# Three feed-forward stages whose down projections take seven half-block products instead of eight

## The chip, the cores and the metric

One core of a Trainium2 chip runs the whole program. The metric is the device time of one execution in microseconds, the median of three runs. A profile of one more execution shows when each engine was busy: PE (TensorE's matmuls), PEld (its weight loads), DVE (VectorE), ACT (ScalarE), POOL (GpSimd) and the DMA queues, of which SP issues most.

## The reference

Two transformer-like blocks on 512 tokens of width 1024, all in float32: first a block with convolution, stick-breaking and cross attention and a feed-forward part, then an attention layer, a convolutional feed-forward layer, a state-space layer and a second convolutional feed-forward layer. The change touches the second matrix of the three feed-forward parts:

```python
# first block: D_FF = 4096
x = x + jnp.square(jax.nn.relu(h2 @ w_up[l])) @ w_down[l]
# each convolutional feed-forward layer: D_FF_2 = 2816
gate, up = jnp.split(h @ w_in, [D_FF_2], axis=-1)
gate = causal_dwconv(gate, conv_w, conv_b)
return (jax.nn.silu(gate) * up) @ w_out
```

## The kernel before

**Matmuls in three parts.** A float32 product is made of three matmuls on rounded halves: each operand is split into a high part (a cast on ScalarE: `act.copy`) and a low part (a subtraction on VectorE: `dve.tensor_sub`), and high*high, high*low and low*high are summed in PSUM. Weights are split on the fly: a load of 1 MB lands in one of two `raw` buffers, and chunks of 128x512 become pairs `whi`, `wlo` in rings of nine (`WB = 9`). So each weight chunk costs one ScalarE and one VectorE instruction of 128x512, beside its matmuls.

**Jobs.** The program is a list of jobs, each a stretch of matmuls. `jobA` makes 256 features for all 512 tokens (48 matmuls), `projB` makes 512 output columns for all tokens out of jobs of four weight chunks (`jobB`: for each tile of 128 tokens, for each k, three matmuls). `run_jobs` goes through the jobs; at each `yield` of a job it emits the low halves that are due (`split_lo`), perhaps the next chunk's high half (`more`, at a rate that `speed` sets, while fewer than nine chunks are in use) and the tasks that are due by a clock of planned times (`pump`). The order in each engine's queue is the order of emission. Tasks are spawned with planned delays and planned engine costs.

**The feed-forward stages.** The first block has four groups of 8 feature tiles (128 features each), each convolutional layer groups of 8, 8 and 6. A group's features come from `jobA`s: in the first block 4 per group, in a convolutional layer 4 (or 3) pairs, one job for the gate and one for the other factor. Each feature tile is 128x512 (features by tokens); `Feat.put` splits it into high and low. The down projection of group g is placed after the first `jobA` (the first pair) of group g+1; the last group's stands at the stage's end, where the normalisation of the next stage hangs on it (`x_done`: sums of squares on ScalarE, transposes on PE, copies on VectorE and ScalarE). It is eight half-block products in effect: 2 column halves, 4 token tiles, 8 (or 6) feature tiles, three matmuls each; each of the two halves ends with four adds of a PSUM bank into the residual `x`.

GpSimd does one product by a 128x512 row per gate tile (`fy<-fy,R`), and little else in these stages.

Of the kernel before, what the change touches and what calls it, by code (L numbers as in the profile page):

```python
# [10 lines left out]
F32R = mybir.dt.float32r  # L11
# [45 lines left out]
class Job:  # L57
    def __init__(self, pieces, nk, nc, run, pre=None):
        self.pieces = pieces
        self.nk = nk  # L60
        self.nc = nc
        self.run = run
        self.pre = pre
        self.speed = 0.6


@with_exitstack
def kernel(ctx: ExitStack, tc: tile.TileContext, ins: dict, out: bass.AP, parts=(1, 2, 3, 4, 5)):
# [107 lines left out]
    def rel(tag):  # L176
        freed[tag].append(max(done[0], now[0]))

    def hand_over():

        live["g"] -= 1
        live["t"] += 1

    def u8(nm, dt=F32):
        return up.tile([128, 2048], dt, tag="u8", name=nm)

    def t2(nm, dt=F32, n=512):
        return tp.tile([128, n], dt, tag="t2", name=nm)
# [49 lines left out]
    def drain():  # L238
        while tasks:
            step()  # L240

    def until(ready):

        limit = now[0] + 500.0
        while not ready():
            if tasks:
                step()
            else:
                now[0] += 0.1
            assert now[0] < limit  # L250
# [39 lines left out]
    WB = 9  # L290

    def load(i):
        if i >= len(jobs) or i in raws:
# [9 lines left out]
    def split_hi(i, c):  # L303

        j = jobs[i]
        if c == 0:
            load(i)
            load(i + 1)
        r = raws[i].rearrange("p k c -> p (k c)")
# [3 lines left out]
        s = r[:, c * w:(c + 1) * w]  # L313
        act.copy(h, s)
        late.append(lambda: dve.tensor_sub(l, s, f(h)))
        split.setdefault(i, []).append((h, l))
        if (c + 1) * w >= j.nk * j.nc:
            raws.pop(i)

    def split_lo():  # L320
        while late:
# [2 lines left out]
    class W:  # L324
# [3 lines left out]
        def get(self, k, c0, c1):  # L328
# [3 lines left out]
            o = (k % kq) * j.nc  # L332
            return h[:, o + c0:o + c1], l[:, o + c0:o + c1]

    def run_jobs():
        chunks = [(i, c) for i, j in enumerate(jobs) for c in range(max(1, j.nk * j.nc // 512))]
        st = {"n": 0, "used": 0}

        def more(limit, upto=None):
            while limit > 0 and st["n"] < len(chunks):  # L340
                i, c = chunks[st["n"]]
                if upto is not None and i > upto:
                    return
                if upto is None and st["used"] >= WB:
                    return
                split_lo()
                split_hi(i, c)
                st["n"] += 1
                st["used"] += 1
                limit -= 1  # L350

        for i, j in enumerate(jobs):
            if j.pre is not None:
                j.pre()
            more(99, i)
            if late and chunks[st["n"] - 1][0] == i:
# [9 lines left out]
            st["used"] -= len(split.pop(i))  # L366
        drain()

    def mm3(ps, sh, sl, mh, ml, first, last):
# [4 lines left out]
    class Feat:  # L374
# [136 lines left out]
    def projB(wap, r0, nk, c0, X, evac, ntt=NT, pre=None, k0=0, cut=None, mid=None):  # L511
        state = {}
        n = 0
        for m in cut or [4] * (nk // 4):
            jobB(wap, r0 + n * 128, m, c0, X, k0 + n, state, n == 0, n + m == nk, evac, ntt, 512,
                 pre if n == 0 else mid)
            n += m


    def rstd_of(ms, n, nm):  # L520
# [40 lines left out]
    def x_half(tt, h):  # L561
        return x_ap(tt)[:, h * 512:(h + 1) * 512]
# [51 lines left out]
    def between(holder):  # L614
        return lambda: holder["row"]()
# [18 lines left out]
    def first_block():  # L634
# [422 lines left out]
        def up_evac(g, k0):  # L1057
            def evac(ft, ps):
                if k0 + ft == 0:
                    F[g] = Feat("ff", KD)  # L1060
                r = t2("r")
                dve.scalar_tensor_tensor(out=r, in0=ps, scalar=0.0, in1=G["R"], op0=ALU.max, op1=ALU.mult)

                def rest():
                    act.activation(out=r, in_=r, func=AF.Square)
                    yield from F[g].put(k0 + ft, r)

                spawn(rest(), 0.8)
            return evac

        def down(g, last):
            for half in range(2):
                projB(ins["w_down"], g * 1024, KD, half * 512, lambda: F[g], residual(half, last),
                      pre=(lambda: hooks.update(x=hooks["next1"])) if last and half == 0 else None)

        for g in range(4):
            for i in range(4):
                jobA(ins["w_up"], g * 1024 + i * 256, lambda: G["h"], up_evac(g, 2 * i),
                     between=between(G) if g == 0 and i == 0 else None)
                if i == 0 and g > 0:  # L1080
                    down(g - 1, False)
        down(3, True)
# [212 lines left out]
    def conv_ffn(layer, G, nxt):  # L1295
        w = ins["ffn_w_in_2"][layer]
        wo = ins["ffn_w_out_2"][layer]
        F = {}
        gt = {}

        def gate_evac(k0):
            def evac(ft, ps):
                k = k0 + ft

                def done(y):
                    pool.tensor_tensor(out=y, in0=y, in1=G["R"], op=ALU.mult)
                    gt[k] = y

                spawn(conv_silu(ps, G["R"], [col(f"fcw{layer}", 3 * k + i) for i in range(3)],
                                col(f"fcb{layer}", k), None, done))  # L1310
                pump()
            return evac

        def up_evac(k0, g, base):
            def evac(ft, ps):
                k = k0 + ft
                if k == base:
                    F[g] = Feat("fs", 8)
                until(lambda: k in gt)
                y = gt.pop(k)  # L1320
                dve.tensor_mul(y, ps, y)
                spawn(F[g].put(k - base, y), 0.9)
            return evac

        def down(g, base, nk, last):
            for half in range(2):
                projB(wo, base * 128, nk, half * 512, lambda: F[g], residual(half, last),
                      cut=[nk - 4, 4],
                      pre=(lambda: hooks.update(x=hooks[nxt])) if last and half == 0 else None)

        groups = ((0, 8), (8, 8), (16, 6))
        X = lambda: G["h"]
        for g, (base, n) in enumerate(groups):
            for i in range(n // 2):
                k0 = base + 2 * i
                jobA(w, k0 * 128, X, gate_evac(k0), between=between(G) if k0 == 0 else None)
# [425 lines left out]
```

## Time and profile before

| | |
|---|---|
| Median of three runs | 2547.79 us (2546.73 to 2548.28) |
| Profiled execution, its own time | 2546.88 us |
| Its span, first to last instruction | 2544.8 us |
| Mean granted TensorE clock | 0.995 |
| PE busy | 98% of the span, 11732 matmuls |
| DVE, ACT, POOL busy | 59%, 41%, 10% |

Busy times of an engine are unions of its instructions. A chain of waits is followed back from the last instruction. An engine that is off the chain may still decide when others can start.

### The profile page before, as it was taken

What the parts mean: (1) busy time and instruction counts of PE and PEld (TensorE: products, weight loads), DVE (VectorE), ACT (ScalarE), POOL (GpSimd) and SP (SyncE); (2) the same over time, 40 slices, a digit from 0 to 9 for tenths busy, and PEclk for the clock granted to TensorE, in tenths of its full rate; (3) what the DMA queues carried; (4) which work ended last, traced back from release to release, by engine and by line L of the source; (5) the groups of instructions that cost most, each with busy time, mean ns of one, the idle gap of its engine ahead of it and who ended that gap; (6) DMA issues with size and microseconds to landing.
All of it is one profiled execution on the core that took longest, in us unless ns stands there. A gap on an engine that the chain in (4) does not pass through costs nothing.

```text
span 2544.8 us, 30656 instructions
## 1 busy us (share of the span) xinstructions
PE 2494.2 (98%) x11732; PEld 2015.6 (79%) x11732; DVE 1509.6 (59%) x2752; ACT 1054.7 (41%) x2242; POOL 253.0 (10%) x292
## 2 busy tenths in 40 slices
PE   8999999999999999999898999999999998999999
PEld 6777777788888888888676888888778886888887
DVE  6435679953445443346867654646688687764644
ACT  6444565632224332234555332223565544432321
POOL 1000111201110000002210110100011011110100
PEclk9999999999999999999999999999999998999999
DMA  5212222233232332332121232322332431322232
GB/s 203 100 66 87 96 67 67 67 124 102 90 134 94 103 99 83 99 100 75 44 100 34 96 103 83 116 75 93 114 96 83 124 108 58 100 95 90 98 100 83
DMA packets 197394, 238.54 MB, mean 94 GB/s; under 512 B 5856, under 2 KB 148576, under 8 KB 197248
## 3 DMA queue, kind: packets, MB, share of 16 engines
q1 hardware_dynamic: 194224, 230.17, 27.7%
q10 hardware_dynamic: 3024, 6.42, 0.7%
q8 instruction: 92, 1.51, 0.2%
q14 instruction: 54, 0.44, 0.1%
HBM read 232.31 MB, written 4.26 MB: 93 GB/s over the span
## 4 chain that ended last, share of the span: by engine, by line
PE 91%; DVE 6%; ACT 1%; issue 1%; DMA 1%; POOL 1%; SPq 0%; ACTq 0%; DVEq 0%; POOLq 0%
PE ga L83 48%; PE gb L83 33%; PE y L83 1%; PE z L83 1%; PE as L83 1%; PE tr L88 1%; PE o L83 1%; DVE wlo L116 1%; PE aT L88 1%; DVE ae L116 1%; DVE sm L116 1%; DVE fy L116 1%; PE xs L83 1%; PE xo L83 1%; PE ao L83 0%
## 5 line engine op out<-in xcount | busy, mean ns | idle before, releaser
L116 DVE TENSOR_TENSOR wlo<-raw,whi 128x512 fp32r<-128x512 f32 (+1 forms) x813 | 578.7, 735 | 220.5 <-ACT whi L116 219.8
L83 PE MATMUL ga<-hh,whi 128*128 128x512 f32 x1672 | 668.0, 400 | 0.0
L83 PE MATMUL ga<-hh,wlo 128*128 128x512 f32 x1672 | 652.9, 390 | 2.1 <-DVE wlo L116 2.1
L83 PE MATMUL ga<-hl,whi 128*128 128x512 f32 x1672 | 652.1, 390 | 0.0
L116 ACT CAST whi<-raw 128x512 fp32r<-128x512 f32 (+1 forms) x813 | 479.1, 616 | 317.1 <-PE gb L83 212.2
L83 PEld LDWEIGHTS ga<-hh,wlo 128*128 128x128 f32 x1672 | 313.6, 188 | 70.4 <-DVE wlo L116 2.9
L83 PEld LDWEIGHTS ga<-hh,whi 128*128 128x128 f32 x1672 | 313.9, 188 | 68.9 <-issue 4.4
L83 PEld LDWEIGHTS ga<-hl,whi 128*128 128x128 f32 x1672 | 313.9, 188 | 66.3 <-issue 2.2
L116 DVE TENSOR_TENSOR x<-gb,x 128x512 f32<-128x512 f32 x136 | 93.9, 690 | 274.4 <-PE gb L83 273.1
L83 PE MATMUL gb<-whi,hh 128*128 128x512 f32 (+1 forms) x416 | 169.5, 408 | 0.0
L83 PE MATMUL gb<-whi,hl 128*128 128x512 f32 (+1 forms) x416 | 159.4, 383 | 0.0
L83 PE MATMUL gb<-wlo,hh 128*128 128x512 f32 (+1 forms) x416 | 159.1, 382 | 0.3 <-DVE wlo L116 0.3
L83 PE MATMUL gb<-whi,fsh 128*128 128x512 f32 x352 | 137.7, 391 | 0.0
L83 PE MATMUL gb<-whi,fsl 128*128 128x512 f32 x352 | 137.0, 389 | 0.0
L83 PE MATMUL gb<-wlo,fsh 128*128 128x512 f32 x352 | 137.0, 389 | 0.0
L116 ACT ACTIVATE fy<-fy,cols 128x512 f32<-128x512 f32 x60 | 43.5, 725 | 183.6 <-DVE fy L116 183.6
L116 POOL TENSOR_TENSOR fy<-fy,R 128x512 f32<-128x512 f32 x44 | 62.1, 1411 | 575.6 <-ACT fy L116 570.0
L116 DVE SCALAR_TENSOR_TENSOR fy<-fg,cols,fy 128x510 f32<-128x510 f32 (+1 forms) x136 | 104.6, 769 | 4.8
L83 PE MATMUL gb<-whi,ffh 128*128 128x512 f32 x256 | 100.4, 392 | 0.0
L83 PE MATMUL gb<-whi,ffl 128*128 128x512 f32 x256 | 99.7, 389 | 0.0
L83 PE MATMUL gb<-wlo,ffh 128*128 128x512 f32 x256 | 99.7, 389 | 0.0
L116 DVE TENSOR_TENSOR fg<-ga,R 128x512 f32<-128x512 f32 x68 | 46.6, 685 | 84.4 <-PE ga L83 73.5
(271 smaller groups left out, 3703.3 us busy)
## 6 DMA issues: line engine op xcount, KB each, us to landing
raw<-in_ffn_w_in_dram SPq DMA_DIRECT2D x44, 1024.0 KB, 4.9
raw<-in_w_in_dram SPq DMA_DIRECT2D x40, 1024.0 KB, 4.9
raw<-in_ffn_w_out_dram SPq DMA_DIRECT2D x20, 1024.0 KB, 4.9
raw<-in_w_up_dram SPq DMA_DIRECT2D x16, 1024.0 KB, 5.3
raw<-in_w_down_dram SPq DMA_DIRECT2D x16, 1024.0 KB, 4.9
raw<-in_ssm_w_in_dram SPq DMA_DIRECT2D x16, 1024.0 KB, 5.0
raw<-in_attn_w_in_dram SPq DMA_DIRECT2D x9, 1024.0 KB, 5.0
raw<-in_w_mem_kv_dram SPq DMA_DIRECT2D x8, 1024.0 KB, 5.1
```

Source lines behind the costliest of these rows:

```text
L83: nc.tensor.matmul(o, lhsT=lhsT, rhs=rhs, **kw)
L88: nc.tensor.transpose(o, i, idn)
L116: return fn(*args, **kw)
```

## The change

Each group's down projection is written as a product of 2x2 blocks: tokens in halves of 256 (two tiles), features in halves of nk/2 tiles, columns in halves of 512. Seven products of half blocks give the four output blocks, with sums and differences of blocks as operands. Each product is 4 (or 3) feature tiles by 2 token tiles by three matmuls.

- `seven` replaces the two `projB` of a group by seven jobs. The four quarter blocks of the weight are loaded once, two into `raw`, two into buffers of the `u8` pool (`big`). After a chunk of product 0, 1, 2 or 3 is split, a sum of 128x512 of two quarter blocks is made in place (`j.after = mix(...)`), so that a later product finds its operand there. All 7x4 (7x3) chunks are split into high and low.
- `Hidden` replaces `Feat` for the features: they are kept unsplit, and `operands` makes each product's left operand in two tasks, one per pair of feature tiles: for four of the seven a sum of 128x512, for all seven a cast on ScalarE and a subtraction on VectorE of 128x512. At most three operands stand at a time (`NOP`). `work()` spawns them at the start of the `jobA` (the pair) that precedes the down projection.
- Sums go through `add_on`, which takes GpSimd unless, by planned times, VectorE would be free more than 1 us earlier (`lighter(pool, dve, 1.0)`).
- After each product two PSUM banks (256 tokens by 512 columns) are added into `x`: seven times two adds per group, where there were eight. Banks are kept over several products.

```diff
+def lighter(a, b, more):
+    return b if max(b.free, now[0]) + more < a.free else a
...
         act.copy(h, s)
         late.append(lambda: dve.tensor_sub(l, s, f(h)))
+        if j.after is not None:
+            late.append(lambda: j.after(c))
...
+    SEVEN = (("11", "e"), ("s1", "c"), ("s2", "e"), ("s4", "c"), ("s3", "e"), ("12", "f"), ("22", "e"))
+    NOP = 3
+    def add_on(out, a, b, op):
+        lighter(pool, dve, 1.0).tensor_tensor(out=out, in0=a, in1=b, op=op)
...
+        def operands(self, a, b):
...
+                while self.done < i - (NOP - 1) or not all(
+                        ("r", k + j * self.hk) in self.got for j in need for k in range(a, b)):
+                    yield 0.3
...
+                if name == "s1":
+                    add_on(t, A(2, 1), A(2, 2), ALU.add)
+                elif name == "s2":
+                    add_on(t, t, A(1, 1), ALU.subtract)
+                elif name == "s4":
+                    add_on(t, A(1, 2), t, ALU.subtract)
+                elif name == "s3":
+                    add_on(A(2, 1), A(1, 1), A(2, 1), ALU.subtract)
...
+                act.copy(h, src)
+                yield 0.2
+                dve.tensor_sub(r3(o[:, 1024 + a * 256:1024 + b * 256], b - a), src, f(h))
...
+    def seven(wap, r0, nk, H, last, pre=None):
...
+        def first(i):
+            load(i)
+            R["0"] = flat(raws.pop(i))
+            load(i + 1)
+            R["1"] = flat(raws.pop(i + 1))
+            big("2", 2, 2)
+        def mix(out, a, b):
+            return lambda c: add_on(*[R[x][:, c * 512:(c + 1) * 512] for x in (out, a, b)], ALU.subtract)
...
+                for n, (k, t) in enumerate(order):
+                    wh, wl = wt.get(k, 0, 512)
+                    h, l = H().at(name, k)
+                    h, l = (x[:, t * 128:(t + 1) * 128] for x in (h, l))
+                    ps = banks[bk, t]
+                    s, e = new and k == 0, k == hk - 1
+                    pe.matmul(ps, lhsT=h, rhs=wh, start=s, stop=False, skip_group_check=True)
+                    pe.matmul(ps, lhsT=h, rhs=wl, start=False, stop=False, skip_group_check=True)
+                    pe.matmul(ps, lhsT=l, rhs=wh, start=False, stop=e, skip_group_check=True)
...
+                for t in range(2):
+                    tt = 2 * (row - 1) + t
+                    xa = x_half(tt, half)
...
+                    dve.tensor_add(xa, banks[bk, t], xa)
...
+                    if fin and last:
+                        x_done(tt, half)
+                yield
...
+        srcs = ("0", "0", "0", "2", "1", "3", "0")
+        sums = (("0", "1", "0"), ("0", "2", "0"), ("1", "2", "1"), ("0", "3", "0"), None, None, None)
...
+            j.speed = 1.2
...
-                    yield from F[g].put(k0 + ft, r)
+                    act.activation(out=F[g].slot(k0 + ft), in_=r, func=AF.Square)
...
         def down(g, last):
-            for half in range(2):
-                projB(ins["w_down"], g * 1024, KD, half * 512, lambda: F[g], residual(half, last), ...
+            seven(ins["w_down"], g * 1024, KD, lambda: F[g], last, ...
...
-                dve.tensor_mul(y, ps, y)
-                spawn(F[g].put(k - base, y), 0.9)
+                dve.tensor_mul(F[g].slot(k - base), ps, y)
+                F[g].got.add(("r", k - base))
```

## Rows read from the trace of the kernel before

**Rows 1.** The page's first part: busy us, share of the span, instructions.
```profile
PE 2494.2 (98%) x11732; PEld 2015.6 (79%) x11732; DVE 1509.6 (59%) x2752; ACT 1054.7 (41%) x2242; POOL 253.0 (10%) x292
```
**Rows 2.** The chain of waits in order of time: start us, us, what.
```profile
859.00 43.52 PE gb L83 x192
902.52 43.52 PE ga L83 x192
...
2464.38 43.52 PE ga L83 x192
2507.90 32.65 PE gb L83 x144
2540.58 0.69 DVE x L116
```
**Rows 3.** Busy us by stretch (x instructions), then PEclk, DMA share, GB/s.
```profile
core 0: us, PE busy (x) PEld busy (x) DVE busy (x) ACT busy (x) POOL busy (x), PEclk, DMA share, GB/s
859.00:902.50 43.50, 43.50 (x193) 36.02 (x193) 15.93 (x25) 12.17 (x20) 0.00 (x0) 1.00 0.25 82
902.50:946.00 43.50, 43.50 (x194) 36.02 (x193) 20.00 (x31) 16.07 (x28) 0.00 (x0) 1.00 0.35 111
1109.00:1158.00 49.00, 49.00 (x239) 40.78 (x238) 25.20 (x42) 18.53 (x40) 1.36 (x3) 1.00 0.27 90
1559.00:1646.00 87.00, 87.00 (x386) 72.03 (x385) 54.61 (x79) 25.79 (x45) 11.22 (x8) 1.00 0.32 105
```
**Rows 4.** Timeline of DVE around a gate job and its partner: start us, us.
```profile
1556.17 0.69 DVE L116 TENSOR_TENSOR x<-gb,x 128x512 f32<-128x512 f32 x1 [1.43 <-PE gb L83]
1556.78 1.29 DVE L116 TENSOR_TENSOR wlo<-raw,whi 128x512 fp32r<-128x512 f32 x2
...
1564.33 0.69 DVE L116 TENSOR_TENSOR fg<-ga,R 128x512 f32<-128x512 f32 x1 [4.15 <-PE ga L83]
1565.06 0.48 DVE L116 TENSOR_SCALAR fy<-fg,cols 128x512 f32<-128x512 f32 x1
1565.58 1.54 DVE L116 SCALAR_TENSOR_TENSOR fy<-fg,cols,fy 128x511 f32<-128x511 f32 x2
1567.03 2.98 DVE L116 TENSOR_TENSOR wlo<-raw,whi 128x512 fp32r<-128x512 f32 x3
...
1727.60 0.69 DVE L116 TENSOR_TENSOR fy<-ga,fy 128x512 f32<-128x512 f32 x1 [1.97 <-PE ga L83]
1728.21 1.28 DVE L116 TENSOR_TENSOR wlo<-raw,whi 128x512 fp32r<-128x512 f32 x2
```
**Rows 5.** Timeline of POOL over the same places.
```profile
1567.95 1.52 POOL L116 TENSOR_TENSOR fy<-fy,R 128x512 f32<-128x512 f32 x1 [58.39 <-ACT fy L116]
1573.55 1.29 POOL L116 TENSOR_TENSOR fy<-fy,R 128x512 f32<-128x512 f32 x1 [4.08 <-ACT fy L116]
...
1726.98 1.29 POOL L116 TENSOR_TENSOR fy<-fy,R 128x512 f32<-128x512 f32 x1 [5.19 <-ACT fy L116]
```
**Rows 6.** Timeline of DVE and POOL in the state-space stage, both busy.
```profile
1944.61 2.13 DVE L116 TENSOR_TENSOR m<-m,bc 128x512 f32<-128x512 f32 x2
1944.70 1.50 POOL L116 TENSOR_TENSOR y<-sx,cols 128x512 f32<-128x512 f32 x1
1946.16 1.49 POOL L116 TENSOR_TENSOR stt<-stt,et 128x512 f32<-128x512 f32 x1
1946.67 1.53 DVE L116 TENSOR_TENSOR xw<-xdt,tok 128x512 f32<-128x512 f32 x1
1947.61 1.49 POOL L116 TENSOR_TENSOR y<-sx,cols 128x512 f32<-128x512 f32 x1
1948.12 2.13 DVE L116 TENSOR_TENSOR m<-m,bc 128x512 f32<-128x512 f32 x2
```
**Rows 7.** Instructions of tile wlo: duration ns min/median/max.
```profile
L116 DVE TENSOR_TENSOR wlo<-raw,whi x813: 427/685/1790, 8.0 to 2524.9; 128x512 fp32r<-128x512 f32 x163
```
**Rows 8.** Groups by form: busy us, mean ns of one, idle before.
```profile
L116 ACT CAST whi<-raw 128x512 fp32r<-128x512 f32 x812 | 478.7, 617 | 317.1 <-PE gb L83 212.2 <-DMA raw<-in_ffn_w_in_dram 33.5 <-PE ga L83 21.2
```
**Rows 9.** The page's DMA issues: KB each, us to landing.
```profile
raw<-in_w_down_dram SPq DMA_DIRECT2D x16, 1024.0 KB, 4.9
```

More of the change, by code (lines that the diff above doesn't have):

```diff
@@ L64, in __init__ @@
         self.speed = 0.6
+        self.source = None
+        self.after = None
+        self.prefetch = None
 @with_exitstack
@@ L292, in load @@
     def load(i):
-        if i >= len(jobs) or i in raws:
+        if i >= len(jobs) or i in raws or jobs[i].pieces is None:
             return
@@ L305, in split_hi @@
         j = jobs[i]
-        if c == 0:
+        if c == 0 and j.prefetch is not None:
+            j.prefetch(i)
+        elif c == 0:
             load(i)
             load(i + 1)
-        r = raws[i].rearrange("p k c -> p (k c)")
         w = min(512, j.nk * j.nc)
@@ L333, in get, with done @@
             return h[:, o + c0:o + c1], l[:, o + c0:o + c1]
+        def done(self):
+            freed_chunks[0] += 1
+    freed_chunks = [0]
     def run_jobs():
@@ L343, in more @@
                     return
-                if upto is None and st["used"] >= WB:
+                if upto is None and st["used"] - freed_chunks[0] >= WB:
                     return
@@ L366, in run_jobs @@
             st["used"] -= len(split.pop(i))
+            freed_chunks[0] = 0
         drain()
@@ new lines, in seven, with big, flat, source @@
+    def seven(wap, r0, nk, H, last, pre=None):
+        hk = nk // 2
+        w = hk * 512
+        R, banks = {}, {}
+        block = lambda i, j: wap[r0 + (i - 1) * hk * 128:r0 + i * hk * 128, (2 - j) * 512:(3 - j) * 512]
+        def big(nm, i, j):
+            R[nm] = u8("b" + nm)
+            sp.dma_start(out=r3(R[nm][:, 0:w], hk), in_=block(i, j).rearrange("(k p) c -> p k c", p=128))
+        def flat(t):
+            return t.rearrange("p k c -> p (k c)")
+        def first(i):
[6 more added lines that the diff above has]
+            return lambda c: add_on(*[R[x][:, c * 512:(c + 1) * 512] for x in (out, a, b)], ALU.subtract)
+        def source(nm):
+            return lambda c: R[nm][:, c * 512:(c + 1) * 512]
+        def product(i):
+            name, bk = SEVEN[i]
+            def run(wt):
+                quota[0] = 4
+                new = i in (0, 1, 5)
+                if new:
+                    for t in range(2):
+                        banks[bk, t] = bank("g", "gw")
+                order = [(k, t) for k in range(hk) for t in range(2)]
+                if last and i == 6:
+                    order = [(k, t) for t in range(2) for k in range(hk)]
+                for n, (k, t) in enumerate(order):
[7 more added lines that the diff above has]
+                    pe.matmul(ps, lhsT=l, rhs=wh, start=False, stop=e, skip_group_check=True)
+                    if n % 2 and n + 1 < len(order):
+                        if order[0][1] != order[1][1]:
+                            wt.done()
+                        yield
+                H().done += 1
+                row, half, fin = ((1, 1, 0), (2, 0, 0), (1, 0, 0), (1, 0, 1), (2, 0, 1), (1, 1, 1), (2, 1, 1))[i]
+                for t in range(2):
+                    tt = 2 * (row - 1) + t
+                    xa = x_half(tt, half)
+                    over = i in (3, 5, 6)
+                    if over:
+                        hand_over()
+                    dve.tensor_add(xa, banks[bk, t], xa)
+                    if over:
+                        rel("t")
+                    if fin and last:
+                        x_done(tt, half)
+                yield
+            return run
+        srcs = ("0", "0", "0", "2", "1", "3", "0")
+        sums = (("0", "1", "0"), ("0", "2", "0"), ("1", "2", "1"), ("0", "3", "0"), None, None, None)
+        n0 = len(jobs)
+        for i in range(7):
+            pieces = {0: [(0, 512, block(1, 1))], 1: [(0, 512, block(1, 2))]}.get(i)
+            j = Job(pieces, hk, 512, product(i), pre if i == 0 else None)
+            j.speed = 1.2
+            j.source = source(srcs[i])
+            if sums[i]:
+                j.after = mix(*sums[i])
+            j.prefetch = {0: first, 1: lambda i: big("3", 2, 1), 6: lambda i: load(i + 1)}.get(i, lambda i: None)
+            jobs.append(j)
@@ L1064, in rest @@
                 def rest():
-                    act.activation(out=r, in_=r, func=AF.Square)
-                    yield from F[g].put(k0 + ft, r)
+                    act.activation(out=F[g].slot(k0 + ft), in_=r, func=AF.Square)
+                    F[g].got.add(("r", k0 + ft))
+                    yield
                 spawn(rest(), 0.8)
@@ L1071, in down @@
         def down(g, last):
-            for half in range(2):
-                projB(ins["w_down"], g * 1024, KD, half * 512, lambda: F[g], residual(half, last),
-                      pre=(lambda: hooks.update(x=hooks["next1"])) if last and half == 0 else None)
+            seven(ins["w_down"], g * 1024, KD, lambda: F[g], last,
+                  pre=(lambda: hooks.update(x=hooks["next1"])) if last else None)
         for g in range(4):
             for i in range(4):
+                ready = {(1, 0): 0, (2, 0): 1, (3, 0): 2, (3, 3): 3}.get((g, i))
                 jobA(ins["w_up"], g * 1024 + i * 256, lambda: G["h"], up_evac(g, 2 * i),
-                     between=between(G) if g == 0 and i == 0 else None)
+                     between=between(G) if g == 0 and i == 0 else None,
+                     pre=None if ready is None else lambda ready=ready: F[ready].work())
                 if i == 0 and g > 0:
@@ L1317, in evac @@
                 if k == base:
-                    F[g] = Feat("fs", 8)
+                    F[g] = Hidden("fs", groups[g][1])
                 until(lambda: k in gt)
                 y = gt.pop(k)
-                dve.tensor_mul(y, ps, y)
-                spawn(F[g].put(k - base, y), 0.9)
+                dve.tensor_mul(F[g].slot(k - base), ps, y)
+                F[g].got.add(("r", k - base))
             return evac
         def down(g, base, nk, last):
[L1326 to L1329, printed above, removed]
+            seven(wo, base * 128, nk, lambda: F[g], last,
+                  pre=(lambda: hooks.update(x=hooks[nxt])) if last else None)
         groups = ((0, 8), (8, 8), (16, 6))
@@ L1335, in conv_ffn @@
                 k0 = base + 2 * i
-                jobA(w, k0 * 128, X, gate_evac(k0), between=between(G) if k0 == 0 else None)
+                ready = {(1, 0): 0, (2, 0): 1, (2, 2): 2}.get((g, i))
+                jobA(w, k0 * 128, X, gate_evac(k0), between=between(G) if k0 == 0 else None,
+                     pre=None if ready is None else lambda ready=ready: F[ready].work())
                 jobA(w, FF2 + k0 * 128, X, up_evac(k0, g, base))
```

47 lines of the change are left out of this document (44 added, 3 removed).

## The prediction

> **What bounds the kernel now.** I read the page's shares first: TensorE is busy 98% of the span, VectorE 59%, GpSimd 10% [rows 1]. Then the chain of waits in order of time, in the stages that change: a down projection of a group of 8 stands there as one unbroken piece of 192 matmuls in 43.52 us, one of 6 as 144 in 32.65 us, and the pieces of features between them are just as dense [rows 2]. So a matmul costs 43.52 / 192 = 0.2267 us wherever it stands, and nothing but the number of matmuls sets the time there. The table by stretch shows what cover the other engines have: VectorE is busy 15.9 of 43.5 us in a down projection, 20.0 of 43.5 in the feature jobs of the first block, 25.2 of 49.0 where the next stage's normalisation is prepared, 54.6 of 87.0 in the feature jobs of a convolutional layer; GpSimd has nothing to do in the down projections [rows 3].
>
> **What the change removes.** A group of 8 has 7 x 24 = 168 matmuls for 192, one of 6 has 126 for 144. Four groups in the first block, two of 8 and one of 6 in each convolutional layer: 8 x 24 + 2 x 18 = 228 matmuls, at 0.2267 us 51.7 us (5.44 and 4.08 us a group). Order and banks of the matmuls change, but feature jobs, which change bank every 6 matmuls, have the same rate as down projections, which do it every 12 [rows 2]; I cost that at nothing. Loads stay the same four quarter blocks.
>
> **What it adds, per group of 8.** On ScalarE 28 weight casts for 16 and 14 operand casts for 8, 18 x 0.62 = 11 us [rows 8]; ScalarE was busy 12.2 of 43.5 us [rows 3], so this stays covered, at nothing. On VectorE 12 more low halves of weights, 6 more of operands and 6 more residual adds (14 for 8). On GpSimd or VectorE 24 sums of 128x512: 16 of quarter blocks, 8 for operands. All of it falls in the down projection and the feature job or pair just before it, since three operands at most stand ready and the weights are split about five chunks ahead.
>
> **What a VectorE instruction costs.** Back to back, starts are 0.60 us apart where both inputs are in SBUF (two take 1.29, one lasts 0.69), and 0.61 for an add that reads PSUM (1556.17 to 1556.78); the four instructions of a gate tile take 2.70 us (1564.33 to 1567.03) [rows 4]. The Trainium skill (VectorE: DVE Perf Modes, the section on the TRN2 errata) gives (N+151)/0.96 for an fp32 tensor_tensor, 691 ns at 512. That is how long one lasts here, not how often one can start; with it the 32 instructions of the worst stretch below would cost 2.9 us more a group, some 29 us in all. The sum goes by 0.60.
>
> **What a sum on GpSimd costs VectorE.** This decides. GpSimd's product at 1567.95 takes 1.52 us and VectorE's three subtractions beside it 2.98 us, where they would take 0.69 + 2 x 0.60 = 1.89: VectorE lost 1.09 us [rows 4, 5]. The longest subtraction in the whole trace, 1790 ns against a median of 685, is of this kind [rows 7]. Where both engines have a queue, in the state-space stage, they take turns: GpSimd starts at 1944.70, 1946.16 and 1947.61, one VectorE instruction between each, so a pair takes 1.46 and VectorE loses 1.46 - 0.60 = 0.86 [rows 6]. Beside a VectorE instruction that reads PSUM nothing is lost (1727.60 lasts its 0.69, GpSimd's at 1726.98 its 1.29, as when VectorE is idle at 1573.55) [rows 4, 5]. So the price lies between 0 and 1.09 us of VectorE's time per sum, when VectorE itself would make it in 0.60. In the worst stretch VectorE is never idle and 1.2 of some 9 us are residual adds, which read PSUM: I take 0.86 x 0.87 = 0.75. Of 24 sums I give GpSimd 20, as its planned lag of 1 us passes some on; each sum moved between the two changes the total by only 0.15.
>
> **The sum, middle groups of the first block.** In a product of 5.44 us VectorE now has 4 weight low halves, 2 operand low halves (6 x 0.60 = 3.6) and 2 residual adds (1.2), 4.8 us: covered. The sums are not spread over the seven products. Those of quarter blocks follow the splits of products 0 to 3, which run a product ahead: 4 fall in the feature job, 4 in each of products 0 to 2; operand sums are 4 in the feature job, 2 each in products 1 and 2. So the feature job (10.9 us) has 9 instructions and 2 evacuations on VectorE and 6 sums on GpSimd, 5.4 + 1.2 + 4.5 = 11.1, a lag of 0.2. Product 0 has 3.6 + 4 x 0.75 = 6.6; products 1 and 2 have 4.8 + 0.6 + 5 x 0.75 = 9.15 each; product 3 has 4.8. That is 29.9 us from the first product's start. Behind it VectorE, in order, has product 3's residual adds (1.2) before the low half of product 4's last chunk (0.69), and TensorE needs 1.36 for that chunk's six matmuls: product 4 ends at 33.2 us instead of 5 x 5.44 = 27.2. TensorE stalls 6.0 us and does not get them back, for after that it sets the pace: 6.0 - 5.44 = +0.6 a group, three groups +1.8.
>
> **The others.** Middle groups of the convolutional layers have two feature jobs (21.8 us) before: 14 x 0.60 + 2 x 2.70 + 1.2 + 8 x 0.75 (two gate products of GpSimd among them) = 21.0, no lag, and an operand more is ready: 31.8 us, stall 4.6, -0.9 a group, four groups -3.6. The first block's last group feeds the normalisation, two more VectorE instructions (1.2 us) for each of 8 half tiles, 6 of them now in products 4 to 6 at 2.4 a product: VectorE comes to 46.4 us at the end, TensorE with its stall of 6.0 and its transposes to the same, +0.6. The groups of 6 have 3 chunks in 4.08 us, so worse proportions: 4.05, 7.3, 7.3, 4.0 and 3.25 are 25.9 against 20.4, stall 5.5, +1.4; in the first layer, with the normalisation, 37.7 against 31.2, +2.4. Together +1.8 - 3.6 + 0.6 + 1.4 + 2.4 = +2.6 us: the saving is taken back almost to a microsecond. The profiled execution, 2546.88 us (span 2544.8), becomes 2549.5; it lies 0.9 below the median of the runs, so **2551 us** for those.
>
> **Bounds.** Some 18 GpSimd sums stand before the point where a group stalls, so 0.1 us of price is 1.8 us a group, 18 us in all. At 0.42 the stalls are gone; below that nothing more is won. At 1.09 it is +60 us.
>
> **Rivals.** *VectorE keeps up.* GpSimd's instructions fall beside residual adds, evacuations, or moments when VectorE waits for a product to end; its price falls under 0.42 and TensorE runs through. For it: VectorE must wait for TensorE before each pair of residual adds, and 0 was measured beside PSUM readers [rows 4, 5]. Against it: in products 1 and 2 VectorE has no such moment left. It gives 2547.8 - 51.7 and some 8 us where the normalisation crowds the last groups: 2504 us. The Trainium skill (GPSIMD Engine Reference, section 3.1) counts a two-input add on GpSimd as about twice VectorE's time and nothing for VectorE, which would make this the case; its section 1 names the shared SBUF interface without a price, and rows 4 to 6 have the price.
> *VectorE stands in its queue for a load.* The first quarter sums need the second quarter block. It is issued when product 0's first chunk is split and takes 4.9 us to land [rows 9]; the sum follows about 1.4 us behind the split. The plan knows no landing times. Where it passes that sum, or one that needs GpSimd's late result, to VectorE, up to 3.5 us go by with low halves and evacuations queued behind: 35 us over ten groups, 2586 us. Against it: GpSimd is asked first, and is free at that moment unless operand sums stand there. It decides where the first sums fall to VectorE.
> *The forecast*, saving and stalls about even, reaches from 2535 to 2570 (price 0.66 to 0.85).
>
> **Chances.** Forecast 0.46, keeps up 0.28, queue 0.22, the rest (a lower clock in the stalls, the memory of the 14 `u8` buffers) 0.04, on the slow side. 0.2% is about what a measurement of this kernel can tell from no change, 5.1 us: 2542.7 to 2552.9. The forecast gives 0.12 below it, 0.19 in it, 0.15 above. So faster 0.12 + 0.28 = 0.40, same 0.19, slower 0.15 + 0.22 + 0.04 = 0.41. A tenth on either side is left out: 2508 (into the keeping up) to 2592 (past the queue).
>
> **What the profile would show.** Matmuls 11732 - 228 = 11504. In the chain, down projections no longer unbroken: subtractions (`wlo`) and GpSimd's sums between them, in products 1 to 4 and not in 5 and 6 of the middle groups. GpSimd with some 20 more instructions a group at 1.46 to 1.52 us, and `wlo` well over its median of 685 ns [rows 7]. VectorE over 90% busy over products 0 to 3. I am wrong if pieces of 168 matmuls in 38.1 us stand in the chain (keeps up), if VectorE's idle time there is put down to a load or to GpSimd (queue), or if `wlo` lasts 0.69 beside GpSimd's sums.

## The result, and the profile after

The changed kernel takes 2652.95 us (median of four runs, 2650.39 to 2655.25) where the kernel before took 2547.98: a ratio of 1.0413 with an interval of 1.0395 to 1.0431. It is 105 us slower, 102 above the forecast and 61 above the top of its range. The profiled execution has a span of 2648.7 us (2544.8 before) and a mean granted TensorE clock of 0.984 (0.995 before).

The page's first part, the shares of the chain that ended last, and the groups of instructions on which the forecast had put a number:

```profile
PE 2490.3 (94%) x11504; PEld 1982.4 (75%) x11504; DVE 1819.4 (69%) x3038; ACT 1144.9 (43%) x2420; POOL 545.4 (21%) x476
...
PE 72%; DVE 19%; issue 4%; ACT 2%; DMA 2%; POOL 1%; SPq 0%; ACTq 0%; POOLq 0%; DVEq 0%
...
L119 DVE TENSOR_TENSOR wlo<-raw,whi 128x512 fp32r<-128x512 f32 x851 | 671.4, 811 | 199.4 <-ACT whi L119 198.4
...
L119 POOL TENSOR_TENSOR raw<-b,raw 128x512 f32<-128x512 f32 x110 | 178.6, 1650 | 12.5 <-DVE wlo L119 9.8
...
L119 DVE TENSOR_TENSOR x<-gw,x 128x512 f32<-128x512 f32 x140 | 92.7, 684 | 50.1 <-PE gw L86 50.0
```

Against [rows 1] there are the 228 matmuls fewer, as forecast, but TensorE's share has gone from 98 to 94% and VectorE holds 19% of the chain. A sum on GpSimd takes 1.65 us, not 1.46 to 1.52. Of 232 sums 184 went to GpSimd (476 - 292 instructions) and 48 to VectorE, 18.4 to 4.8 a group, near the forecast 20 to 4. Before the residual adds `x<-gw,x` VectorE stood idle 50.0 us, waiting for a product's last matmul; not all of that is loss, for behind products 4 and 5 of the middle groups TensorE runs on without a gap meanwhile.

Where the time went, from the first matmul of each down projection to its last (`gw`; before [rows 2] for the middle groups):

| groups | before | after | change | forecast |
|---|---|---|---|---|
| first block, 3 middle | 43.52 | 52.83, 54.08, 53.14 | +29.5 | +1.8 |
| convolutional, 4 middle | 43.52 | 47.76, 47.68, 47.78, 47.68 | +16.8 | -3.6 |
| first block, last | 46.97 | 66.06 | +19.1 | +0.6 |
| first convolutional, last | 36.09 | 52.98 | +16.9 | +2.4 |
| second convolutional, last | 32.64 | 46.51 | +13.9 | +1.4 |
| together | | | +96.2 | +2.6 |

96.2 of the 103.9 us of span are there. The first middle group by product (boundaries by the first matmul of each; columns as in [rows 3]):

```profile
859.90:865.40 5.50, 5.50 (x26) 4.55 (x25) 5.50 (x6) 3.20 (x7) 4.81 (x4) 1.00 0.01 3
865.40:870.80 5.40, 5.40 (x26) 4.46 (x24) 5.40 (x7) 2.16 (x4) 4.08 (x3) 1.00 0.00 0
870.80:883.70 12.90, 7.67 (x26) 4.96 (x24) 12.90 (x10) 3.98 (x8) 12.90 (x9) 0.88 0.00 0
883.70:894.60 10.90, 7.89 (x26) 5.54 (x25) 9.70 (x12) 5.99 (x11) 3.81 (x3) 0.67 0.00 0
894.60:901.90 7.30, 5.77 (x26) 4.42 (x25) 5.57 (x10) 4.05 (x7) 0.00 (x0) 1.00 0.47 145
901.90:912.80 10.90, 10.90 (x50) 9.03 (x49) 9.38 (x16) 2.49 (x4) 0.00 (x0) 1.00 0.27 78
```

Most signs of the forecast are there: products 5 and 6 (the last row) run without a gap, products 2 to 4 do not (product 1, which the forecast had counted among these, has no gap), VectorE is busy 100% of products 0 to 2. But product 4 ends 42.0 us after product 0's start, where the forecast had 33.2. The chain of waits through it shows how:

```profile
865.67 1.71 DVE wlo L119
867.38 1.20 DVE x L119 x2
...
879.62 1.71 DVE wlo L119
881.33 1.68 DVE wt L119
883.00 0.95 DVE wlo L119
883.96 0.67 issue
884.62 1.76 DVE wlo L119
886.38 1.69 DVE ffs L119
888.07 0.04 issue
888.11 6.61 PE gw L86 x22
894.72 0.02 issue
894.75 0.69 DVE x L119
895.44 0.60 DVE wlo L119
896.04 0.61 DVE ffs L119
896.65 0.04 issue
896.69 16.20 PE gw L86 x70
```

Up to 888.1 the chain is VectorE's own queue, mostly at 1.7 us an instruction, for the sums of GpSimd run beside it. What ends it is `ffs`, the low half of product 3's left operand, a chain of sum (`wt`, on VectorE here), cast and low half. So product 3 had not begun but for two matmuls, and its other 22 follow at one go, in 6.61 us. Then the residual adds, which need its last matmul, stand in VectorE's queue ahead of two low halves that product 4 needs, and TensorE waits again, 894.7 to 896.7. Of the 70 matmuls that follow 48 are those of products 5 and 6, so 22 of product 4's 24 were still to come. VectorE itself stood 1.2 us ahead of these adds:

```profile
890.98 1.88 DVE L119 TENSOR_TENSOR wlo<-raw,whi 128x512 fp32r<-128x512 f32 x3
894.07 1.37 DVE L119 TENSOR_TENSOR x<-gw,x 128x512 f32<-128x512 f32 x2 [1.20 <-PE gw L86]
```

The price of a sum is read from the timelines of GpSimd and VectorE (start us, us):

```profile
869.45 14.71 POOL L119 TENSOR_TENSOR raw<-b,raw 128x512 f32<-128x512 f32 x9 [0.63 <-DVE wlo L119]
```
```profile
871.60 1.77 DVE L119 TENSOR_TENSOR ffs<-wt,ffs 128x512 fp32r<-128x512 f32 x1
873.29 3.44 DVE L119 TENSOR_TENSOR wlo<-raw,whi 128x512 fp32r<-128x512 f32 x2
876.65 1.77 DVE L119 TENSOR_TENSOR wt<-ffr,wt 128x512 f32<-128x512 f32 x1
878.35 1.27 DVE L119 TENSOR_TENSOR x<-gw,x 128x512 f32<-128x512 f32 x2
```

Beside nine sums in a row VectorE's instructions start about 1.70 us apart (871.60, 873.29, then 876.65 two later, 878.35), so each loses 1.70 - 0.60 = 1.10. The two adds that read PSUM take 1.27 for two and lose nothing.

### The profile page after: what moved, and what is told of

Read it like the earlier page. It is cut to its first block, busy times and chain, and to the rows that moved or that the text cites. A ratio compares the mean times of both kernels' runs of the same rounds, so it can differ in the third digit from the quotient of the medians.

```text
span 2648.7 us, 31061 instructions
## 1 busy us (share of the span) xinstructions
PE 2490.3 (94%) x11504; PEld 1982.4 (75%) x11504; DVE 1819.4 (69%) x3038; ACT 1144.9 (43%) x2420; POOL 545.4 (21%) x476
## 4 chain that ended last, share of the span: by engine, by line
PE 72%; DVE 19%; issue 4%; ACT 2%; DMA 2%; POOL 1%; SPq 0%; ACTq 0%; POOLq 0%; DVEq 0%
PE ga L86 41%; PE gb L86 16%; PE gw L86 7%; DVE wlo L119 7%; DVE x L119 2%; DVE fss L119 2%; PE y L86 1%; PE z L86 1%; DVE wt L119 1%; DVE ffs L119 1%; DVE fy L119 1%; PE as L86 1%; PE o L86 1%; PE aT L91 1%; DVE ae L119 1%
## 5 line engine op out<-in xcount | busy, mean ns | idle before, releaser
L119 DVE TENSOR_TENSOR wlo<-raw,whi 128x512 fp32r<-128x512 f32 x851 | 671.4, 811 | 199.4 <-ACT whi L119 198.4
L119 ACT CAST whi<-raw 128x512 fp32r<-128x512 f32 x851 | 501.2, 616 | 292.2 <-DMA raw<-in_ffn_w_in_dram 73.4
L119 POOL TENSOR_TENSOR raw<-b,raw 128x512 f32<-128x512 f32 x110 | 178.6, 1650 | 12.5 <-DVE wlo L119 9.8
L86 PE MATMUL gw<-whi,fss 128*128 128x512 f32 x352 | 116.0, 407 | 22.4 <-DVE fss L119 19.2
L119 POOL TENSOR_TENSOR raw<-raw,raw 128x512 f32<-128x512 f32 x38 | 61.6, 1629 | 338.4 <-DMA raw<-in_w_down_dram 169.8
L119 DVE TENSOR_TENSOR x<-gw,x 128x512 f32<-128x512 f32 x140 | 92.7, 684 | 50.1 <-PE gw L86 50.0
L119 ACT ACTIVATE fy<-fy,cols 128x512 f32<-128x512 f32 x60 | 43.5, 725 | 185.2 <-DVE fy L119 185.1
L86 PE MATMUL gw<-whi,ffs 128*128 128x512 f32 x256 | 91.4, 438 | 23.2 <-DVE ffs L119 20.9
L86 PEld LDWEIGHTS gw<-whi,fss 128*128 128x128 f32 x352 | 66.5, 193 | 44.0 <-DVE fss L119 27.4
L86 PE MATMUL gw<-wlo,fss 128*128 128x512 f32 x176 | 73.4, 417 | 25.8 <-DVE wlo L119 25.4
```

What stands on the lines that cost most here:

```text
L86: nc.tensor.matmul(o, lhsT=lhsT, rhs=rhs, **kw)
L119: return fn(*args, **kw)
```

## The experiments

Each ratio is to the kernel before, run on the same chip; "under after" is the difference to 2653 us. The kernel before took 2546.8 to 2548.2 us in these sessions, so a difference between two runs is good to about 1.5 us.

**All sums on VectorE.** The plan and its order stay; only the engine that gets the instruction differs.

```diff
-        lighter(pool, dve, 1.0).tensor_tensor(out=out, in0=a, in1=b, op=op)
+        e = lighter(pool, dve, 1.0)
+        real, e.real = e.real, nc.vector
+        e.tensor_tensor(out=out, in0=a, in1=b, op=op)
+        e.real = real
```

> All 232 sums are made by VectorE, in the same place of the same plan; GpSimd makes none. Shared port (a sum on GpSimd takes 1.10 us of VectorE's time, on VectorE itself 0.60): 184 sums cost 0.50 us less each, 92 us where VectorE is the one that sets the pace, some 17 of a group's 18 sums there; about 2575 us, 2565 to 2590. Rival, VectorE is simply too full in products 0 to 3, and each sum it takes over costs it 0.60 more: up to 110 us slower than the changed kernel, 2700 to 2760. Rival, TensorE waits for GpSimd's late results: faster as well, near 2555; the run with idle GpSimd work tells it from the first.

2615.24 us, ratio 1.0263 (1.0248 to 1.0278): 38 under after, still 67 over before, and outside all three times that were expected. GpSimd's share is a real cost and not the main one. VectorE now has the 35 us rival's wait, at the first quarter sums:

```profile
L119 DVE TENSOR_TENSOR raw<-raw,raw 128x512 f32<-128x512 f32 x38 | 30.2, 794 | 36.1 <-DMA raw<-in_ffn_w_out_dram 17.7 <-DMA raw<-in_w_down_dram 17.5
```

**No sums at all.** `add_on` does nothing; products take a block itself where they would take a sum.

```diff
-        lighter(pool, dve, 1.0).tensor_tensor(out=out, in0=a, in1=b, op=op)
+        pass
...
-                src = {"s1": t, "s2": t, "s4": t, "s3": A(2, 1)}.get(name)
+                src = {"s1": A(2, 1), "s2": A(2, 2), "s4": A(1, 2), "s3": A(2, 1)}.get(name)
```

> The 232 sums are left out (a product takes the block that would have been summed into); seven products, their splits and adds stay. Shared port: VectorE has 4.8 us of work in a product of 5.44 and keeps up in the middle groups; the last groups lose some us to the normalisation: 2500 to 2512 us. Rival, the order of VectorE's queue (residual adds, which wait for the end of a product, stand before the low half of the next product's last chunk) or the other added work stalls TensorE by itself: 2530 or more.

2523.73 us, ratio 0.9907 (0.9890 to 0.9923), between the two expectations. A middle group in the table by stretch, all seven products:

```profile
942.56:980.60 38.04, 38.04 (x169) 31.54 (x168) 31.11 (x50) 19.78 (x36) 0.00 (x0) 1.00 0.16 48
```

All seven middle groups take 38.08 us, 168 x 0.2267: the saving of 5.44 us a group is there, and the added splits and residual adds are covered. The last groups are not dense: 49.3, 41.5 and 30.6 us, for 38.1, 28.6 and 28.6. The chain of waits in the first block's last:

```profile
1116.16 0.70 DVE x L119
1116.86 0.02 issue
1116.88 0.73 ACT junk L119 x3
...
1118.20 0.61 ACT whi L119
1118.83 0.69 DVE wlo L119
```

Behind a product's residual adds the next stage's squares (`junk`) stand in ScalarE's queue ahead of the cast `whi` that the next product waits for.

**Sums on VectorE, and GpSimd adds each result to itself into a scratch tile** that nobody reads, 184 times, where it would have made the sum (the `sm` pool has 10 buffers for 16 to make room).

```diff
+        if e is pool:
+            z = idle[:, 0:a.free_size()]
...
+            nc.gpsimd.tensor_tensor(out=z, in0=out, in1=out, op=ALU.add)
```

> VectorE makes all sums as in the run with all sums on VectorE; behind each of the 184 that GpSimd would have made, GpSimd adds the result to itself into a scratch tile that nobody reads. Nobody waits for GpSimd. Shared port: the 1.10 us a piece come back and the sums' 0.60 stay with VectorE: slower than the changed kernel, 2690 to 2760. Rival, waits for GpSimd's results: the same as with all sums on VectorE, within 10 us of it.

2734.24 us, ratio 1.0734 (1.0718 to 1.0750): 119 over the run with all sums on VectorE, though no matmul needs GpSimd's result.

**The same with a one-input copy.**

```diff
-            nc.gpsimd.tensor_tensor(out=z, in0=out, in1=out, op=ALU.add)
+            nc.gpsimd.tensor_copy(z, out)
```

> As the run with idle GpSimd work, but GpSimd copies the sum (one input) instead of adding it to itself (two inputs). If any GpSimd instruction on SBUF locks out VectorE's two-input instructions for as long as it runs: between 2660 and 2740, by its duration. If only two-input GpSimd instructions do: the same as with all sums on VectorE, 2605 to 2625.

2675.12 us, ratio 1.0498 (1.0483 to 1.0514): 60 over the run with all sums on VectorE. A copy, and the VectorE instruction beside it:

```profile
869.35 0.95 POOL L553 COPY idle<-raw 128x512 f32<-128x512 f32 x1 [1.98 <-DVE raw L119]
```
```profile
869.14 0.69 DVE L119 TENSOR_TENSOR ffs<-wt,ffs 128x512 fp32r<-128x512 f32 x1
869.74 1.10 DVE L119 TENSOR_TENSOR wlo<-raw,whi 128x512 fp32r<-128x512 f32 x1
```

VectorE's low half takes 1.10 for 0.69: it loses 0.41 to a copy. Both runs show the price on VectorE where nothing waits for GpSimd's result: no wait of another engine is put down to the scratch tile in either profile. The smaller `sm` pool is the same in both, so it has no part in the 59 us between them.

**Quarter sums without a landing wait**: all operands from the block already there (in this run the sums are doubled blocks).

```diff
-            return lambda c: add_on(*[R[x][:, c * 512:(c + 1) * 512] for x in (out, a, b)], ALU.subtract)
+            return lambda c: add_on(*[R[x][:, c * 512:(c + 1) * 512] for x in (out, out, out)], ALU.add)
```

> Sums stay on GpSimd, but those of quarter blocks take both inputs from the buffer that is there already, so none waits for a quarter block to land (the values are not the reference's). Shared port: the same number of sums beside the same work; two or three of them per group move ahead of product 0, some 3 us a group less stall: 2615 to 2655. Rival, late landings crowd the sums into products 1 to 3 and hold up GpSimd's queue: 2570 or less.

2613.84 us, ratio 1.0260 (1.0245 to 1.0275), 39 under after. But the sums also became shorter, 1370 ns for 1650:

```profile
L119 POOL TENSOR_TENSOR raw<-raw 128x512 f32<-128x512 f32 x148 | 199.7, 1370 | 347.4 <-DVE wlo L119 347.4
```

148 x 0.28 = 41 us of GpSimd's time, so this run, 1 us below the range of the first theory, did not tell the two apart, and the next two were made.

**Early loads, sums by plan**: the second and third quarter blocks are loaded a job or two earlier, into `u8` buffers, the fourth into `raw`.

```diff
-            R["1"] = flat(raws.pop(i + 1))
+            R["3"] = flat(raws.pop(i + 1))
+
+        def early():
+            big("1", 1, 2)
...
```

> The changed kernel with its sums where the plan puts them (184 on GpSimd), and the early loads of the second and third quarter block. Landing as the cause of the 39 us that the run without landing waits gave back: 2605 to 2625. Rival, that run was faster because its sums no longer hang on each other or on a second buffer: 2640 to 2655.

2646.85 us, ratio 1.0389 (1.0373 to 1.0404): 6 under after, as the rival had it. Waiting for loads costs some 6 us there.

**Early loads, all sums on VectorE**: the diffs of the first run and of the one before this together.

> All sums on VectorE as before, and the second and third quarter blocks are loaded into buffers of the u8 pool a job or two earlier (the fourth takes the place in raw), so no sum waits for a landing. In the run with all sums on VectorE it stood 36 us in its queue for those loads. Late landing as the cause of that part: 36 us come back, 2570 to 2590. Rival, VectorE's work alone sets the time and the wait only moves: 2605 to 2616.

2602.28 us, ratio 1.0214 (1.0197 to 1.0231): 13 under late loads, short of what was expected and near the rival. Middle groups still take 45.9 to 47.6 and 43.5 us, though VectorE waits only 2.6 us in all ahead of its quarter sums: 24 sums on VectorE alone stall TensorE by 7.9 to 9.5 us, and 5.4 us, over the 38.08.

**The same with eight products in the three last groups.**

```diff
+            if not last:
+                Q[g] = seven(ins["w_down"], g * 1024, KD, lambda: F[g], last)
+                return
+            for half in range(2):
+                projB(ins["w_down"], g * 1024, KD, half * 512, lambda: F[g], residual(half, last),
...
```

> Seven products only in the seven groups that have a successor, with all sums on VectorE and early loads; the three last groups of the stages take eight half-block products as in the kernel before. If the last groups lose by the normalisation, they are back at their old time and what remains is VectorE's load in the middle groups, between -1 and +1.5 us each: 2540 to 2558. If the loss is spread evenly over all groups: 2565 or more.

2573.44 us, ratio 1.0100 (1.0085 to 1.0115): 29 under the last run, and short of what was expected. The three last groups are back at their old times, but a neighbour got worse (the first block's third group from 47.6 to 56.0, the second group of each convolutional layer from 43.5 to 47.0). The last group's features, now split early, use VectorE and `u8` buffers there, which may be why; this was not shown. This mix of seven and eight does not beat the kernel before either.

**No sums, and the normalisation's work of a last group held back to its last product.**

```diff
-                        x_done(tt, half)
+                        over_tiles.append((tt, half))
+                if i == 6:
+                    for tt, half in over_tiles:
+                        x_done(tt, half)
```

> The run without sums, and the last groups' work for the next stage (squares, transposes, copies; the output's stores in the last layer) is called only behind the seventh product, so ScalarE's squares no longer stand ahead of the casts of the next product. If that queue order stalls the last groups: their products 4 to 6 fall to 5.44 and 4.08 us as in the middle groups, and up to 10 us come back behind the last product of the first two stages: 2505 to 2525 in all. Rival, the last groups are short of operands because their features are late: products 4 to 6 stay over 7 us and the time rises to 2530 or more.

2518.62 us, ratio 0.9884 (0.9869 to 0.9899). The last groups fall from 49.3, 41.5 and 30.6 us to 38.6, 31.3 and 30.5, but of these 21 us only 5 remain in the total: the squares, transposes and copies then stand behind the last product with nothing beside them. **The same with early loads and sums on VectorE:**

> All sums on VectorE, early loads, and the last groups' work for the next stage only behind the seventh product. Queue order in the last groups: products 4 to 6 there fall back to 5.44 and 4.08 us, some 22 us, of which the exposed normalisation takes most again, as without sums (5 us net): 2588 to 2600. Rival, the last groups are held by VectorE's load, not by the order: products 4 to 6 stay long and the time is 2602 or more.

2600.99 us, ratio 1.0209 (1.0194 to 1.0225), between the two expectations. The last groups of the first two stages fall from 60.8 to 50.1 and from 50.9 to 44.0 us, the third, where the late work is the output's stores, rises from 41.0 to 45.1, and the total falls by 1.3, which is no more than the sessions differ. The normalisation costs about the same inside the products as behind them.

**Early loads, sums on VectorE, and no residual adds after products 0, 1 and 2** (60 adds left out).

```diff
-                    dve.tensor_add(xa, banks[bk, t], xa)
+                    if i > 2:
+                        dve.tensor_add(xa, banks[bk, t], xa)
```

> All sums on VectorE, early loads, and the residual adds behind products 0, 1 and 2 left out (6 of a group's 14; the output lacks three partial blocks). If VectorE's instructions set the pace in products 2 to 4, each 0.60 us taken away there comes back: 60 adds, up to 36 us, 2566 to 2580. Rival, the chain from a sum to its cast, its subtraction and the matmul is what TensorE waits for, whatever VectorE does beside it: 2595 to 2603.

2545.89 us, ratio 0.9994 (0.9985 to 1.0004): 56 us for 60 adds, which are 60 x 0.605 = 36 us of work. That is below both expectations. An add costs more than its own time; middle groups fall to 39.95 and 38.9. Part of the 20 us above the count may be the clock: matmuls that start 0.30 to 0.52 us before the next in the down projections cost some 26 us over 0.2267 with the adds and some 13 without. No wait of TensorE is put down to a residual add itself, with them or without.

**A fourth matmul per token tile and weight chunk in products 1 to 3.**

```diff
+                    if i in (1, 2, 3):
+                        nc.tensor.matmul(ps, lhsT=l, rhs=wh, start=False, stop=False, skip_group_check=True)
                     pe.matmul(ps, lhsT=l, rhs=wh, start=False, stop=e, skip_group_check=True)
```

> In products 1, 2 and 3 of every group the low*high matmul is issued twice (so their blocks hold that term twice); planned order and all other engines stay as in the changed kernel. TensorE gets 24 x 3 = 72 more matmuls in each of eight groups and 18 x 3 = 54 in the two of 6: 3 x 228 = 684 ... of which the third part is new, 8 a product: 8 x 3 x 8 + 6 x 3 x 2 = 228, just the number that the change had removed, 51.7 us at 0.2267. Theory, VectorE's queue sets the pace in these products: TensorE waits there some 115 us over the ten groups, so the new matmuls fall into the waits, and only those of the last two pairs before a product's residual adds are felt, at most 2 x 0.23 = 0.45 us in each of 30 products: 2653 + 0 to 13.6, so 2653 to 2667. Rival, the lower granted clock in these products is itself a good part of the loss: 180 matmuls there start at over 0.3 us from the next, 29 us more than at 0.2267; a busier TensorE would keep the clock, and the time falls below 2650, down to 2635. Rival, TensorE at its lower clock sets the pace in these products: 228 x 0.2267 to 228 x 0.43, 2705 to 2750.

2663.74 us, ratio 1.0459 (1.0441 to 1.0476): 51.7 us more of matmuls cost 11. Middle groups of the convolutional layers take 47.7 to 47.8 us with or without the 24 matmuls more; what is lost lies in the first block's groups and in the last ones. Products 2 and 3 of one, after and then here:

```profile
1577.95:1588.73 10.78, 6.64 (x26) 4.19 (x24) 10.78 (x8) 4.88 (x9) 10.78 (x8) 1.00 0.00 0
1588.73:1597.38 8.65, 6.29 (x26) 4.28 (x25) 8.65 (x12) 2.35 (x5) 3.17 (x2) 1.00 0.00 0
```
```profile
1584.17:1592.64 8.47, 7.56 (x33) 5.93 (x32) 8.47 (x8) 4.03 (x8) 8.47 (x6) 1.00 0.01 2
1592.64:1602.88 10.24, 7.88 (x33) 5.85 (x32) 10.24 (x13) 3.43 (x7) 4.29 (x3) 1.00 0.00 0
```

VectorE is busy every moment of both, TensorE is not: VectorE sets the pace. The granted clock is 1.00 in both, so here it has no part in the loss.

## Why the prediction was wrong

**What held.** Nothing but the number of matmuls sets the time of a covered down projection: 38.08 us without sums. ScalarE's and VectorE's added splits are covered in the middle groups without the sums. GpSimd got 18 sums a group; TensorE stalls in products 2 to 4 of the middle groups and not in 5 and 6, for lack of VectorE's results; the shared access of GpSimd and VectorE is what sums on GpSimd pay with.

**The step that failed first: how a full VectorE queue reaches TensorE.** The sum added up VectorE's work over products 0 to 3 (29.9 us) and let TensorE end product 4 two residual adds, one low half and six matmuls later (3.3 us). By that sum a price of 0.60 in place of 0.75, for 18 sums in ten groups, would save 27 us: 2524. (By its own stretches 14 sums of GpSimd stand in products 0 to 2 and six in the feature job, where they count only as it lags; 18 lies between. And 2549.5 + 0.9 is 2550.4, where it wrote 2551.) With every sum on VectorE at 0.60 the chip gave 2615, and with no landing waits 2602, 78 over. So the larger part of the error is not the price.

Nor is it the amount of work at that price. At 0.60 the forecast's stretches come to 6.0 + 8.4 + 8.4 + 4.8 = 27.6 us, and in the run with all sums on VectorE and early loads VectorE came to product 3's residual adds 27.5 us after product 0's start (949.9, second middle group). What failed is what stands behind. The chain of waits from there:

```profile
977.38 1.20 DVE x L119 x2
978.58 0.60 DVE wlo L119
979.18 0.61 DVE ffs L119
...
979.84 16.16 PE gw L86 x70
```

Behind the adds comes the low half of product 4's left operand (`ffs`), for which all of that product but its first two matmuls waits: 22 were left (70 less the 48 of products 5 and 6), not six. Product 4 ends 7.6 us behind the start of the adds, at 985.0, where the sum had 3.3. In the changed kernel's group above it is the same at 888.1 for product 3 and at 896.7 for product 4. There VectorE had worked 33.0 us when it was done with all ahead of the adds, 3 more than forecast, and product 4 ended 9.0 us later: 1.2 standing for product 3's last matmul, which came 1.6 late by the clock (below), then two adds, two low halves and 22 matmuls. Sixty adds less gave back 56 us, where a count of their work gives 36, or 49 with all that the clock can have given back.

**The price was mis-sized too.** 0.86 in a queue came from [rows 6], where a pair takes 1.46; here a pair takes 1.70 and VectorE loses 1.10, which is the upper bound read from [rows 4, 5]. From product 0's start to 888.1 VectorE made 23 instructions in 28.2 us; 23 x 0.60 = 13.8, so 15 sums cost it 0.96 each with those beside PSUM readers, where I took 0.75. The GpSimd instructions of [rows 6] are shorter (1.49 and 1.50 for a mean of 1.65). At the bound the prediction itself gave +60, 2608 us, 45 short of what was measured. The swap of engine alone is worth 2653 - 2615 = 38 us (2646.85 - 2602.28 = 45 with early loads), much less than 184 x (1.10 - 0.60) = 92. Part of the sums may fall where VectorE waits anyway; that was not shown. The Trainium skill (Perfetto Trace Analysis, Optimizing Scalar/DVE Operations) says that moving work between these two engines may not help, since they share a read port. These runs agree, and say how much: it hurts by 38 us.

**The last groups** were forecast at +4.4 together and took +49.9: 45.5 of the 93.6 us by which the down projections miss the forecast lie in these three, 48.1 in the seven middle ones. Without sums they take 121.4 us, 26 over dense products but only 6 over the kernel before, with the squares in ScalarE's queue in front of casts; I had counted the normalisation as VectorE work only. Held back, it costs nearly the same behind the group. The sums add the other 44 us, 14.7 a group, where a middle group loses 12.1 to them.

**The rivals.** VectorE keeping up is what happens without sums (2524), not with them. Standing in the queue for a load exists, but at 13 us on VectorE and 6 on GpSimd, not 35. The lower clock, in the 0.04 of the rest, is real in the first block and some last groups.

**The way from 2548 to 2653**, as steps between runs: seven products without sums and with the normalisation last, 2518.6 (-29); the normalisation in the products, 2523.7 (+5); the sums on VectorE, loads early, 2602.3 (+79); loads late, 2615.2 (+13); 184 of the sums on GpSimd, 2653 (+38).

**Open.** Of the 8 us of the span that lie outside the down projections, 1.1 come ahead of the first group, 2.2 and 4.4 between the last group of the first and of the second stage and the next down projection; they were not followed further. Why a sum on GpSimd is shorter when both inputs are the same block (1.37 for 1.65 us) was only seen. The clock's share was bounded, not measured. No run put the left operand's low half ahead of the residual adds; that would try the order by itself, and leaving adds out comes nearest to it.

## What to carry to other kernels

Spare time of an in-order engine is not a sum over a stretch: before filling it, follow which of its instructions wait for the engine that it feeds, which of those behind them a whole product hangs on, and place the new work against those, for what stands behind such a wait is late by the wait too. Work on GpSimd is not off VectorE's account when both read SBUF: price it at what a VectorE instruction with two SBUF inputs was seen to lose beside it (here 1.10 us a sum), less where VectorE reads from PSUM meanwhile. A cut in matmuls that pays with operand sums needs cover for the sums where they fall (here 24 per 168 matmuls, most in three of seven products), and is best tried first with the sums left out, to see what there is to win (24 us of the 51.7).

## What the runs showed of the hardware

- GpSimd's two-input add of 128x512 in float32 and a VectorE instruction with both inputs in SBUF take turns: 1.70 us a pair, VectorE loses 1.10. A one-input copy also blocks: 0.95 us, VectorE loses 0.41. VectorE's adds from PSUM lose nothing (two in 1.27). The Trainium skill (GPSIMD Engine Reference, section 1) names the shared interface; the prices are these runs'.
- Some stalled products get a lower clock. In the first middle group the granted clock is 0.88 and 0.67 in products 2 and 3, after waits of up to 3 us (0.50 from 881.4 to 888.1); in the stalled products 2 and 3 of the convolutional group above it stays at 1.00. Matmuls of TensorE in that stretch:

```profile
881.38 0.79 PE L86 MATMUL gw<-wlo,ffs 128*128 128x512 f32 x1 [2.96 <-DVE wlo L119]
881.97 1.05 PE L86 MATMUL gw<-whi,ffs 128*128 128x512 f32 x2
...
888.11 1.22 PE L86 MATMUL gw<-whi,ffs 128*128 128x512 f32 x2 [2.56 <-DVE ffs L119]
889.13 0.63 PE L86 MATMUL gw<-wlo,ffs 128*128 128x512 f32 x1
889.56 1.05 PE L86 MATMUL gw<-whi,ffs 128*128 128x512 f32 x2
...
891.35 0.39 PE L86 MATMUL gw<-wlo,ffs 128*128 128x512 f32 x1
```

From 881.4 to 891, outside the waits, a matmul starts 0.43 us after the one before, about twice 0.2267: the lower of the clock's two levels, 1.2 of 2.4 GHz. So 22 matmuls took 6.61 us where 22 x 0.2267 = 5.0. In all down projections 180 matmuls start between 0.30 and 0.52 us before the next, 28.6 us over 0.2267. That is an upper bound on what the clock cost, since TensorE, had it run them faster, would in part only have waited longer for VectorE; with the fourth matmul it is 144 and 23.8 us, and the total did not fall. A stall in a dense stretch can cost more than its length.
